# A planned matmul kernel on one core: first x tiles in half rows, w1 ahead of w2, and smaller steps for the sums

## The chip, the core and the metric

The kernel runs on one core of one Trainium2 chip, in one launch. The metric is the device time of that core in microseconds (us), as a median over runs. Three runs of the kernel before gave 298.87, 298.88 and 298.90 us.

The engines are named as the profile names them: PE does the matmuls and PEld its weight loads, DVE (VectorE), ACT (ScalarE) and POOL (GpSimd) work on tiles, SP and POOL issue the DMAs here.

## What is computed

```
x: 16 x 512 x 1024, w1 and w2: 1024 x 768, all float32
y1 = x @ w1 ; y2 = x @ w2
out = tanh(y1) * y2          (float32)
```

Flattened, x has 8192 rows, which are 64 tiles of 128 rows ("tile 0" to "tile 63").

## The kernel before

**Two ways to multiply.** The inner dimension of 1024 is cut into 8 chunks k of 128. The columns are cut into three blocks of 512: a is the first 512 columns of w1, b the first 512 of w2, and G the last 256 columns of both side by side. Tiles 0 to 3 ("the head") are multiplied plainly, 8 matmuls of 128x512 for each tile and block (line 522, `m0a4` for tile 0, block a, chunk 4). That makes 4 tiles x 2 blocks + 3 tiles x 1 block, 88 plain matmuls; block b of tile 3 is held back and done as 16 matmuls of 128x256 at the very end. Tiles 4 to 63 go in 20 triples. In a triple the three tiles, each cut in two halves of the inner dimension, and the six weight blocks (three column blocks by two halves) are combined by a fast scheme: 15 products `p0` to `p14` (line 550, 4 matmuls of 128x512 each) instead of 18. Its operands are sums of x blocks (`A_SUMS`, L16, formed by `x_sum`, L505, named `S34.0` for triple 0) and sums of weight blocks (`B_SUMS`, L20, formed once by `w_sum`, L493, named `B5`). The results are added up by `C_OPS` (L29): `copy` and `seed` on ACT, `add` on DVE, then tanh on ACT and the product with y2 on DVE.

**The head.** The loads are float32. `SP_LOADS` and `ACT_LOADS` (L97, L99) list their order: `y0` is the whole of x tile 0 (512 KB), `u3` chunk 3 of w1 (384 KB), `v3` chunk 3 of w2. Each is cast to float16 on DVE or ACT (`cast_y` L417, `cast_w` L431). The x tiles of the head and tiles 4, 5 and 6 are transposed on PE (L463, 8 transposes of 128x128 for each tile, 56 in all) and copied out of PSUM. Later x tiles are loaded as float16 by POOL's DMAs (L471) and transposed by DMAs that SP issues (L474).

**What sets the order.** The whole program is straight-line code. A class `Planner` (L103) takes every step as an `op` with the engines that may do it, a duration, what it needs and a due time, and plays the run forward; the order in which it starts the steps is the order in which the instructions are written, engine by engine. The order of the products is a list (`plan.strict`, L612, from `PE_ORDER` and `PE_HEAD`); the other due times are worked out backward from it. Since each engine takes its instructions in order, a step that comes late holds what stands behind it.

**Fillers.** Matmuls of constants (L857) keep PE busy before the first data (`WARM`, L90) and ahead of four named steps (`FILLERS`, L91).

**The guard.** ACT sums |x| of every tile and |w| of every chunk (`abs_sum`, L476; the x sums are `D0` to `D63`, L814 and L830). Five small steps (`f1` to `f5`, L844) turn the sums into a flag, and after the last product a branch takes a general path if an input is out of range; it is not taken here.

Of the kernel before, what the change touches and what calls it, by code (L numbers as in the profile page):

```python
# [17 lines left out]
    (51, 16, 35, "add"), (15, 11, 4, "sub"), (31, 16, 15, "sub"), (63, 31, 32, "add"), (21, 10, 31, "add"),  # L18
)
B_SUMS = (  # L20
# [5 lines left out]


# [51 lines left out]
PE_HEAD = ("1a0 0a1 1b1 0b1 1G1 p7 p1 0a0 3a0 2b1 p6 0G0 2a1 1b0 1G0 3a1 "  # L79
           "p10 3G1 0b0 p9 p12 2G1 p8 1a1 p11 p14 2b0 0G1 3G0 2G0 2a0")  # L80
# [9 lines left out]
WARM = (512, 512, 256)  # L90
FILLERS = {"PT1.0": (512,), "m1b2": (192,), "m1b7": (256,), "PT2.1": (448,)}  # L91
# [4 lines left out]
EARLY_LOADS = {0: 0.2}  # L96
SP_LOADS = ("y0 y1 v7 u3 y2 u1 v4 u0 v0 "  # L97
            "v1 v3 u2 u4 v5 v6 u6 u5 u7")
ACT_LOADS = "y3 v2"  # L99
POOL_LOADS = "5.0:v5 4.0 4.1 5.1 6"  # L100


class Planner:  # L103
# [221 lines left out]
    def spare(self, n):  # L325

        t = self.start_of[n]
        return [b for b in range(len(self.held)) if all(t <= a or z <= t - 1.0 for a, z in self.held[b])][0]
# [3 lines left out]
def kernel(  # L332
# [27 lines left out]
    XF_BUFS, XG_BUFS = 3, max((SP_LOADS + ACT_LOADS).count("y"), 1)  # L360
# [13 lines left out]
    xtpool = pool("xt", XT_BUFS)  # L374
    spool = pool("s", S_BUFS)
# [14 lines left out]
    xt_last = once.tile([P, KO, P], f16, name="xT_last")  # L390

# [6 lines left out]
    xgpool = head_stack.enter_context(tc.tile_pool(name="xg", bufs=XG_BUFS))  # L398
# [10 lines left out]
    x32, wfs, xhs, xts, ss, cs, os_ = {}, {}, {}, {}, {}, {}, {}  # L409

    def load_x32(e, mt, halves):
        if mt not in x32:
            x32[mt] = xfpool.tile([P, K], f32, tag="xf", name="x_f")
        at = slice(halves[0] * F, (halves[-1] + 1) * F)
        pin(engine[e].dma_start(x32[mt][:, at], xf[mt][:, at]))  # L415

# [30 lines left out]

    def xt_tile(mt):
        if mt not in xts:
            xts[mt] = xt_last if mt == HEAD - 1 else xtpool.tile([P, KO, P], f16, tag=f"xT{mt % 3}", name="xT")  # L450
        return xts[mt]

    def transpose_32(e, mt, h, chain):
        for k in range(KH):
            pin(nc.tensor.transpose(bank(chain)[:, k * P:(k + 1) * P], x32[mt][:, (h * KH + k) * P:(h * KH + k + 1) * P], ident))
# [16 lines left out]

    def transpose(e, mt):
        pin(nc.sync.dma_start_transpose(xt_tile(mt), xhs[mt]))  # L474
# [4 lines left out]
    def abs_x(e, mt):  # L479
        abs_sum(e, xhs[mt] if mt in xhs else x32[mt], mt)  # L480
# [11 lines left out]

    def w_sum(e, v, a, b, how):  # L493
# [5 lines left out]
    def x_operand(i, v):  # L499
        if v & (v - 1):  # L500
            return ss[i, v]
        bit = v.bit_length() - 1
        return xts[HEAD + 3 * i + bit // 2][:, bit % 2 * KH:(bit % 2 + 1) * KH, :]

    def x_sum(e, i, v, a, b, how):  # L505
        ss[i, v] = spool.tile([P, KH, P], f16, tag=f"s{v}", name=f"s{v}")
        pin(engine[e].tensor_tensor(ss[i, v], x_operand(i, a), x_operand(i, b), OP[how]))  # L507
# [11 lines left out]
    def mm(e, chain, mt, k, c, lo, n):  # L519
        begun[chain] = begun.get(chain, 0) + 1  # L520
        w = w_columns(k, c, lo, n)
        pin(nc.tensor.matmul(shaped(bank(chain)[:, lo:lo + n], w), xts[mt][:, k, :], w, start=begun[chain] == 1, stop=begun[chain] == KO, skip_group_check=True))  # L522

    def plain_tanh(e, mt, lo, n, chain):
        pin(nc.scalar.activation(out_tile(mt)[:, lo:lo + n], bank(chain)[:, :n], ACT.Tanh))
# [5 lines left out]
    def steady_pools(e):  # L531
        head_stack.close()
        steady["c"] = fast.enter_context(tc.tile_pool(name="c", bufs=C_BUFS, reuse_waits="tile"))

# [50 lines left out]
    def gate_x(e, mt):  # L585
        pin(nc.gpsimd.tensor_copy(held_x, xts[mt][:, 0, :1]))  # L586
# [8 lines left out]
    ACT_F, ACT_G, ACT_W, ACT_D, ACT_AW = (0.50, 0.59), (0.29, 0.38), (0.80, 0.86), (1.06, 1.26), (0.94, 1.04)  # L595
    PERIOD = 15 * SLOT
# [3 lines left out]
    head_at = {entry: HEAD_START + n * SLOT for n, entry in enumerate(head)}  # L600
    ORIGIN = HEAD_START + (len(head) - 15) * SLOT
# [25 lines left out]
    parts, early, last, back = {}, set(), "", []  # L627
    both = sorted([(ISSUE_ACT * z, "act", z, n) for z, n in enumerate(act_loads)] + [(ISSUE_SP * z, "sp", z, n) for z, n in enumerate(sp_loads)])
    issuer, last_on = {}, {"act": "", "sp": ""}
    for _, e, z, n in both:  # L630
# [3 lines left out]
        if n[1] == "y":  # L634
            mt = int(n[2])
            op(n, {e: (0.49, 0.49) if e == "sp" else (ISSUE_ACT, 0.5) if n != act_loads[-1] else (ISSUE_ACT + TABLE, 0.5)}, -100, [], load_x32, mt, (0, 1), issued=[last], behind=back[-WF_BUFS:][:1] if len(back) >= WF_BUFS else [],
# [3 lines left out]
            for h in range(2):  # L640
# [3 lines left out]
                early.add(f"T{mt}.{h}")  # L644
        elif n[1] == "x":
            z = n[2:]
            mt = int(z[0])
            halves = (int(z[2]),) if z[1:] else (0, 1)
# [7 lines left out]
        else:  # L656
            c, k = n[1], int(n[2])
            op(n, {e: (0.49, 0.49) if e == "sp" else (ISSUE_ACT, 0.5) if n != act_loads[-1] else (ISSUE_ACT + TABLE, 0.5)}, -100, [], load_w, c, k, issued=[last], behind=back[-WF_BUFS:][:1] if len(back) >= WF_BUFS else [],
               dma=(e, 0.985 + more, 1.15, 0.75, 0.121))
# [31 lines left out]
    def loads_of(mt):  # L691
        if mt not in parts:
            return [f"L{mt}"]
        return [n for n in sp_loads + act_loads if n[:3] in (f"Lx{mt}", f"Ly{mt}")] if mt < HEAD else ["L" + part(mt, k)[1:] for k in (0, KO - 1)]

    xt_readers = {mt: [] for mt in range(MT)}


    outs = {mt: [] for mt in range(MT)}
    for c in "aGb":  # L700
        for mt in range(HEAD):
            chain = (c, mt)
            if c == "b" and mt == HEAD - 1:
                continue
            last = []
            for n, k in enumerate(K_ORDER):
                w = [f"c{z}{k}" for z in {"a": "u", "b": "v", "G": "uv"}[c]]
                name = f"m{mt}{c}{k}"
                op(name, {"pe": (MM, MM)}, head_at[f"{mt}{c}{k // KH}"] + n % KH * MM, w + [part(mt, k)], mm, chain, mt, k, c, 0, F, chains=[chain])
                last.append(name)  # L710
            xt_readers[mt] += last
            due = max(head_at[f"{mt}{c}{h}"] for h in range(2)) + MUL_DUE
            if c == "a":
                op(f"th{mt}a", {"act": ACT_F}, due, last, plain_tanh, mt, 0, F, chain, chains=[chain])
            elif c == "G":
                op(f"th{mt}G", {"act": ACT_G}, due, last, plain_tanh, mt, F, G, chain, chains=[chain])
                op(f"mu{mt}G", {"dve": DVE_G}, due, last + [f"th{mt}G"], plain_mul, mt, F, G, chain, G, chains=[chain])
                outs[mt].append(f"mu{mt}G")
            else:
                op(f"mu{mt}b", {"dve": DVE_F}, due, last + [f"th{mt}a"], plain_mul, mt, 0, F, chain, 0, chains=[chain])  # L720
                outs[mt].append(f"mu{mt}b")
# [7 lines left out]
    def w_needs(v):  # L729
        return [f"B{v}"] if v in wsum else casts(v)  # L730

    for v, a, b, how in B_SUMS:
        op(f"B{v}", {"dve": DVE_B}, None, w_needs(a) + w_needs(b), w_sum, v, a, b, how)

    def x_needs(i, v):
        if v & (v - 1):
            return [f"S{v}.{i}"]
# [3 lines left out]
    op("pools", {"pool": (0.0, 0.0)}, 24, back + [f"D{mt}" for mt in range(HEAD)], steady_pools)  # L741
# [8 lines left out]
    for v, a, b, _ in A_SUMS:  # L750
        for u in (a, b):
            if u in a_readers:
                a_readers[u].append(f"S{v}")
# [12 lines left out]
    for i in range(TRIPLES):  # L766
        for v, a, b, how in A_SUMS:
# [212 lines left out]
```

## Time and profile before

| what | value |
|---|---|
| median of three runs | 298.88 us |
| profiled execution, first to last instruction (its span) | 297.3 us |
| PE busy | 290.9 us (98% of the span) |
| DVE busy | 255.5 us (86%) |
| ACT busy | 227.6 us (77%) |
| POOL busy | 46.7 us (16%) |
| HBM read / written | 39.85 MB / 25.17 MB |

The profile is of one execution, and its span of 297.3 us is the only time that it has of its own; the median of the timed runs is 1.6 us above it, which lies around the span. A change of the span is taken as the same change of the time. A busy PE is not a PE at its best: the matmul records overlap, so a matmul's rate is read from how far apart the starts are, not from its length, and constants count as busy.

### The profile page before, as it was taken

How to read it: one execution, taken by the hardware profiler on the slowest of the kernel's cores; microseconds unless marked ns; L12 is line 12 of the kernel's file. 1: busy time of each engine (PE TensorE's matmuls, PEld its weight loads, DVE VectorE, ACT ScalarE, POOL GpSimd, SP SyncE). 2: the span in 40 equal slices, each digit the busy share in tenths (PEclk: the TensorE clock that was granted, in tenths of full speed). 3: DMA queues.
4: the chain of work that ended last, by engine and by line, in shares of the span. 5: the costliest groups of instructions: out<-in, count | busy, mean ns of one | idle time of the engine just before them, and what ended most of it. 6: DMA issues, size and time to landing. Idle time of an engine off the chain costs nothing.

```text
span 297.3 us, 4698 instructions
## 1 busy us (share of the span) xinstructions
PE 290.9 (98%) x1419; PEld 137.7 (46%) x1419; DVE 255.5 (86%) x517; ACT 227.6 (77%) x450; POOL 46.7 (16%) x122
## 2 busy tenths in 40 slices
PE   6999999999999999999999999999999999999995
PEld 3545444444444675444444444444444444444443
DVE  1458999999988999898899988989899898999685
ACT  3798988996969769697876979788696866867561
POOL 1024040211030111113121010212101030000000
PEclk9999999999999999999999999999999999999999
DMA  7999999999999999999999999999989899681316
GB/s 263 406 403 230 162 169 222 242 251 258 110 317 212 221 255 244 221 215 259 161 227 217 172 223 199 246 224 215 226 169 245 164 279 244 144 240 47 119 55 215
DMA packets 82827, 64.55 MB, mean 217 GB/s; under 512 B 62704, under 2 KB 64752, under 8 KB 82800
## 3 DMA queue, kind: packets, MB, share of 16 engines
q1 hardware_dynamic: 73584, 47.59, 62.6%
q0 software_dynamic: 8928, 15.73, 34.3%
q10 hardware_dynamic: 288, 0.92, 0.8%
q8 instruction: 11, 0.18, 0.3%
q14 instruction: 16, 0.13, 0.1%
HBM read 39.85 MB, written 25.17 MB: 219 GB/s over the span
## 4 chain that ended last, share of the span: by engine, by line
PE 91%; DMA 6%; ACT 1%; SPq 0%; DVE 0%; issue 0%
PE bank L550 87%; DMA w_f<-in_w_dram 4%; PE bank L522 3%; DMA x_f<-in_x_dram 2%; ACT wh L427 1%; PE bank L463 1%; SPq L423 0%; DVE o_last L529 0%; SPq L415 0%; PE bank L580 0%
## 5 line engine op out<-in xcount | busy, mean ns | idle before, releaser
L550 PE MATMUL bank<-b,s 128*128 128x512 f16 (+1 forms) x664 | 148.1, 371 | 0.0
L550 PEld LDWEIGHTS <-s 128*128 128x128 f16 x832 | 81.2, 98 | 91.4 <-DVE s L507 0.6
L553 ACT ACTIVATE s<-bank 128x512 f32<-128x512 f32 x100 | 58.6, 595 | 41.0 <-PE bank L550 40.5
L560 DVE TENSOR_TENSOR bank<-bank,s 128x512 f32<-128x512 f32 x100 | 69.5, 697 | 18.1 <-PE bank L550 7.8
L477 ACT ACTIVATE junk<-xh 128x1024 f16<-128x1024 f16 x64 | 67.3, 1051 | 0.2
L567 DVE TENSOR_TENSOR o<-o,bank 128x512 f32<-128x512 f32 (+1 forms) x120 | 63.1, 548 | 2.5 <-ACT o L563 1.7
L550 PEld LDWEIGHTS <-xT 128*128 128x128 f16 x412 | 40.3, 98 | 46.1 <-ACT xT L427 0.2
L550 PE MATMUL bank<-b,xT 128*128 128x512 f16 (+1 forms) x252 | 58.5, 369 | 0.0
L563 ACT ACTIVATE o<-bank 128x256 f32<-128x256 f32 (+1 forms) x80 | 33.0, 432 | 12.4 <-PE bank L550 6.1
L550 PE MATMUL bank<-wh,s 128*128 128x512 f16 (+1 forms) x168 | 41.1, 369 | 0.0
L550 PE MATMUL bank<-wh,xT 128*128 128x512 f16 x160 | 40.9, 379 | 0.0
L586 POOL COPY held_x<-xT 128x1 f16<-128x1 f16 x52 | 12.2, 235 | 165.1 <-DMA xT<-xh 165.0
L471 POOL DMA_DIRECT2D xh<-in_x_dram x62 | 33.3, 540 | 20.3 <-issue 6.6
L507 DVE TENSOR_TENSOR s<-s,xT 128x512 f16<-128x512 f16 x80 | 32.3, 421 | 1.2
L563 ACT ACTIVATE o<-s 128x512 f32<-128x512 f32 x40 | 24.9, 623 | 1.2 <-DVE s L560 1.2
L507 DVE TENSOR_TENSOR s<-xT 128x512 f16<-128x512 f16 x60 | 25.0, 418 | 0.0
L553 ACT ACTIVATE bank<-bank 128x512 f32<-128x512 f32 x40 | 21.7, 573 | 1.6 <-DVE bank L560 0.9
L522 PE MATMUL bank<-wh,xT 128*128 128x512 f16 x72 | 18.8, 378 | 0.3
L507 DVE TENSOR_TENSOR s<-xT,s 128x512 f16<-128x512 f16 x40 | 16.7, 417 | 0.0
L560 DVE TENSOR_TENSOR bank<-s,bank 128x512 f32<-128x512 f32 x20 | 13.9, 694 | 1.6
L560 DVE TENSOR_TENSOR s<-s,bank 128x512 f32<-128x512 f32 x20 | 13.6, 681 | 0.3 <-ACT s L553 0.3
L477 ACT ACTIVATE junk<-wh 128x768 f16<-128x768 f16 x16 | 13.5, 842 | 0.2
(42 smaller groups left out, 120.6 us busy)
## 6 DMA issues: line engine op xcount, KB each, us to landing
out_dram<-o SPq DMA_DIRECT2D x54, 384.0 KB, 4.7
xh<-in_x_dram POOLq DMA_DIRECT2D x58, 256.0 KB, 5.7
w_f<-in_w_dram SPq DMA_DIRECT2D x15, 384.0 KB, 6.3
out_dram<-o SPq DMA_DIRECT2D x9, 256.0 KB, 2.0
x_f<-in_x_dram SPq DMA_DIRECT2D x3, 512.0 KB, 4.7
out_dram<-o SPq DMA_DIRECT2D x9, 128.0 KB, 1.7
xT<-xh SPq DMA_TRANSPOSE x57, 5.3
x_f<-in_x_dram ACTq DMA_DIRECT2D x1, 512.0 KB, 4.9
```

The lines of the kernel that those rows point to most:

```text
L427: pin(nc.scalar.copy(dst, src))
L463: pin(nc.tensor.transpose(b[:, (k - lo) * P:(k - lo + 1) * P], xhs[mt][:, k * P:(k + 1) * P], ident_h))
L471: pin(nc.gpsimd.dma_start(xhs[mt][:, lo * P:(lo + n) * P], xf[mt][:, lo * P:(lo + n) * P]))
L477: pin(nc.scalar.activation(junk[:, :src.shape[-1]], src, ACT.Abs, scale=scale, accum_out=sums[:, column:column + 1]))
L507: pin(engine[e].tensor_tensor(ss[i, v], x_operand(i, a), x_operand(i, b), OP[how]))
L522: pin(nc.tensor.matmul(shaped(bank(chain)[:, lo:lo + n], w), xts[mt][:, k, :], w, start=begun[chain] == 1, stop=begun[chain] == KO, skip_g ...
L550: pin(nc.tensor.matmul(to, x_operand(i, a)[:, k, :], w, start=begins and k == 0, stop=k == KH - 1, skip_group_check=True))
L553: pin(nc.scalar.activation(place(i, dst, True), place(i, src), ACT.Copy, scale=float(sign)))
L560: pin(nc.vector.tensor_tensor(d, a, b, ALU.add if signs == (1, 1) else ALU.subtract))
L563: pin(nc.scalar.activation(out_tile(HEAD + 3 * i + r)[:, lo:lo + n], place(i, src)[:, :n], ACT.Tanh, scale=float(sign)))
L567: pin(nc.vector.tensor_tensor(o, o, place(i, src)[:, at:at + n], ALU.mult))
L586: pin(nc.gpsimd.tensor_copy(held_x, xts[mt][:, 0, :1]))
```

## The change

**Loads.** Tiles 0 to 3 are loaded and cast in half rows: `h3.0` is the first half (chunks 0 to 3) of tile 3, 256 KB. There are 8 of them where there were 4 whole tiles. All 24 loads stand on SP's queue, none on ACT's. The chunks of w1 (u) come ahead of those of w2 (v) but for `v4`, `v7` and `v6`, and tile 2 comes late, behind `v6`.

**Columns.** Block G is no longer one matmul of 128x512 over both weights. Its w1 part is U and its w2 part is V, each 256 wide; a and U read chunks of w1 alone, b and V chunks of w2. Two tiles share a PSUM bank. This makes 64 matmuls of 128x256 out of 32 of 128x512.

**Sums of weights in halves.** `B5`, `B36`, `B37`, `B45` and `B29` are formed in two halves of 256 columns each; the first half needs w1 alone.

**Sums of x in pairs.** `S34` and `S10` are one instruction, `S35` and `S11` another; for that the x tiles and the sums of a triple lie in one tile each (`xTs0`, `ss0`).

**Late sums of |x|.** D0 to D3 are due from 70 us on. D4 to D8 are taken from a second load of tiles 4 to 8, issued on POOL after the last tile's transpose (5 more DMAs of 512 KB read).

**Block b of tiles 0 to 2** is copied out of its bank by ACT, and multiplied by tanh some 30 us later from SBUF.

**Order.** Due times of some 350 steps and the order of the first 41 products are now given as numbers (`DUES`, `FIRST`); the fillers are found by the planner from its own gaps up to its 24 us.

```diff
-PE_HEAD = ("1a0 0a1 1b1 0b1 1G1 p7 p1 0a0 3a0 2b1 p6 0G0 2a1 1b0 1G0 3a1 "
-           "p10 3G1 0b0 p9 p12 2G1 p8 1a1 p11 p14 2b0 0G1 3G0 2G0 2a0")
+PE_HEAD = ("0a1 1a1 2a1 3a1 0U1 1U1 2U1 3U1 0a0 1a0 2a0 3a0 0U0 1U0 2U0 3U0 "
+           "0b1 1b1 2b1 0V1 1V1 2V1 3V1 0b0 1b0 2b0 0V0 1V0 2V0 3V0 p1 p6 p10 p7 p9 p12 p8 p11 p14")
+A_PAIRS = ((34, 10), (35, 11))
+B_HALVES = (5, 36, 37, 29, 45,)
-WARM = (512, 512, 256)
-FILLERS = {"PT1.0": (512,), "m1b2": (192,), "m1b7": (256,), "PT2.1": (448,)}
-SP_LOADS = ("y0 y1 v7 u3 y2 u1 v4 u0 v0 "
-            "v1 v3 u2 u4 v5 v6 u6 u5 u7")
-ACT_LOADS = "y3 v2"
-POOL_LOADS = "5.0:v5 4.0 4.1 5.1 6"
+WARM = (512, 384)
+SP_LOADS = "h3.0 h1.1 h1.0 h0.0 u5 h3.1 h0.1 u7 u0 u1 u2 u4 v4 u3 u6 v7 v6 h2.0 h2.1 v0 v5 v3 v2 v1"
+ACT_LOADS = ""
+HEAD_D_AT, HEAD_D_STEP = 70.0, 9.0
+RELOAD = (4, 5, 6, 7, 8)
+PLAIN_COPY, PLAIN_AT = (0, 1, 2), 30.0
+POOL_LOADS = "4.0:v0 4.1 5.0 5.1 6"
+DUES = ("ch0.1:11.483 PT0.1:-8.806 T0.1:-19.918 ch1.1:-6.643 PT1.1:30.467 T1.1:4.785 cu4:-38.532 ch2.1:7.264 "
...
+    def fillers(self, until):
+        found, busy = {}, None
+        for n in sorted((n for n in self.ops if self.engine_of[n] == "pe"), key=lambda n: self.start_of[n]):
+            t = self.start_of[n]
+            if t > until:
+                break
+            if busy is not None and t - busy > 0.32 and self.spare(n):
+                found[n] = self.spare(n)[0], int((t - busy - 0.18) * 580) // 32 * 32
+            busy = t + self.ops[n]["engines"]["pe"][0]
+        return found
...
+    def load_h(e, mt, h):
+        x32[mt, h] = xfpool.tile([P, F], f32, tag="xf", name="x_f")
+        pin(engine[e].dma_start(x32[mt, h], xf[mt][:, h * F:(h + 1) * F]))
+    def cast_h(e, mt, h):
+        if mt not in xhs:
+            xhs[mt] = xgpool.tile([P, K], f16, tag="xh", name="xh")
+        copy(e, xhs[mt][:, h * F:(h + 1) * F], x32[mt, h])
...
+    def reload_x(e, mt):
+        again[mt] = xhpool.tile([P, K], f16, tag="xh", name="xh")
+        pin(nc.gpsimd.dma_start(again[mt], xf[mt]))
...
+    def w_sum_half(e, v, a, b, how, h):
+        parts_of = [z[:, :, h] if len(z.shape) == 4 else z[:, :, h * G:(h + 1) * G] for z in (wsum[v], w_block(a), w_block(b))]
+        pin(engine[e].tensor_tensor(*parts_of, OP[how]))
...
+    def x_sum(e, i, sums_of):
+        out, a, b = (x_operands(i, [z[n] for z in sums_of]) for n in range(3))
+        pin(engine[e].tensor_tensor(out, a, b, OP[sums_of[0][3]]))
...
-    def mm(e, chain, mt, k, c, lo, n):
+    def mm(e, chain, mt, k, c, lo, n, at, count):
         begun[chain] = begun.get(chain, 0) + 1
-        w = w_columns(k, c, lo, n)
-        pin(nc.tensor.matmul(shaped(bank(chain)[:, lo:lo + n], w), xts[mt][:, k, :], w, start=begun[chain] == 1, stop=begun[chain] == KO, skip_group_check=True))
+        col = N * (c in "bV") + F * (c in "UV") + lo
+        pin(nc.tensor.matmul(bank(chain)[:, at:at + n], xt_tile(mt)[:, k, :], wh[:, k, col:col + n], start=begun[chain] == 1, stop=begun[chain] == count, skip_group_check=True))
...
+    def plain_copy(e, mt, chain):
+        ys[mt] = steady["y"].tile([P, F], f32, tag="y", name="y")
+        pin(nc.scalar.copy(ys[mt], bank(chain)))
+    def plain_mul_copied(e, mt):
+        o = out_tile(mt)[:, :F]
+        pin(nc.vector.tensor_tensor(o, o, ys[mt], ALU.mult))
```

**Place 1: PE at the first plain matmuls.** In the kernel before (`xh` is a cast x tile, `xT` a transposed one, `wh` the cast weights, `ones` the constants), two whole tiles are transposed before these rows:

```order
L463 MATMUL bank5_82<-ident_h_93,xh_167 128x128
L522 LDWEIGHTS xT_151
L522 MATMUL bank6_83<-wh_95,xT_151 128x512
L857 MATMUL bank0_77<-ones_91 128x192
L522 LDWEIGHTS xT_182
L522 MATMUL bank7_84<-wh_95,xT_182 128x512
L857 MATMUL bank0_77<-ones_91 128x256
```

And in the changed kernel, with half tiles (`xTs2` holds tiles 0 to 2, `xT_last` is tile 3):

```order
L553 MATMUL bank3_77<-ident_h_90,xh_166 128x128
L1039 MATMUL bank0_74<-ones_88 128x352
L625 LDWEIGHTS xTs2_94
L625 MATMUL bank4_78<-wh_97,xTs2_94 128x256
L625 MATMUL bank5_79<-wh_97,xTs2_94 128x512
L553 LDWEIGHTS xh_137
L553 MATMUL bank6_80<-ident_h_90,xh_137 128x128
```

The first plain matmuls, a 256-wide one of U and a 512-wide one of a, now stand ahead of the transposes of the second halves of tiles 3 and 0.

**Place 2: PE between the first products of triple 0.** Before, plain matmuls of the head (L522) stand between the products (L550; `s15_394` is a sum of x, `b37_100` one of weights):

```order
L550 MATMUL bank6_83<-b5_97,s15_394 128x512
L522 LDWEIGHTS xT_216
L522 MATMUL bank7_84<-wh_95,xT_216 128x512
L522 LDWEIGHTS xT_last_94
L522 MATMUL bank2_79<-wh_95,xT_last_94 128x512
L550 LDWEIGHTS xT_388
L550 MATMUL bank1_78<-wh_95,xT_388 128x512
```

Now (L625 plain, L662 products, `ss0` the sums of triple 0):

```order
L625 MATMUL bank6_80<-wh_97,xT_last_91 128x256
L662 LDWEIGHTS xTs0_92
L662 MATMUL bank0_74<-wh_97,xTs0_92 128x512
L662 MATMUL bank4_78<-wh_97,xTs0_92 128x512
L662 LDWEIGHTS ss0_95
L662 MATMUL bank3_77<-b24_103,ss0_95 128x512
L662 MATMUL bank7_81<-b5_99,ss0_95 128x512
```

All plain matmuls but those held for the end stand ahead of the first product, and nothing plain is left between products.

**Place 3: DVE ahead of the sum S15 of triple 1**, which product `p6` of that triple reads. Before (`s15_526`; `s34_517` is S34 of triple 1):

```order
L507 TENSOR_TENSOR s11_508<-s3_493,xT_402 128x512
L507 TENSOR_TENSOR s34_517<-xT_418,xT_385 128x512
L567 TENSOR_TENSOR o_467<-o_467,bank4_81 128x256
L507 TENSOR_TENSOR s15_526<-s11_508,xT_402 128x512
L497 TENSOR_TENSOR b45_102<-b37_100,wh_95 128x2048
```

Now (the rows of 128x1024 are pairs, `45_104` of 128x4x256 is a half sum of weights, and the last row is S15):

```order
L610 TENSOR_TENSOR ss1_96<-xTs1_93 128x1024
L589 TENSOR_TENSOR b45_104<-b37_102,wh_97 128x4x256
L610 TENSOR_TENSOR ss1_96<-ss1_96,xTs1_93 128x1024
L672 TENSOR_TENSOR bank0_74<-bank4_78,s56_518 128x512
L679 TENSOR_TENSOR o_485<-o_485,bank2_76 128x256
L679 TENSOR_TENSOR o_485<-o_485,bank1_75 128x512
L610 TENSOR_TENSOR ss1_96<-ss1_96,xTs1_93 128x512
```

S15 now stands behind an add and two output products, where one output product of 256 columns stood before.

More of the change, by code (lines that the diff above doesn't have):

```diff
@@ L479, in abs_x @@
     def abs_x(e, mt):
[L480 removed]
+        abs_sum(e, again[mt] if mt in again else xhs[mt], mt)
     def abs_w(e, t, k):
@@ L868 @@
             o = plan.ops[n]
-            for z in FILLERS.get(n, ()):
-                constants(banks[plan.spare(n)], z)
+            if n in fillers:
+                b, z = fillers[n]
+                for at in range(0, z, F):
+                    constants(banks[b], min(F, z - at))
             o["fn"](plan.engine_of[n], *o["args"])
```

208 lines of the change are left out of this document (146 added, 62 removed), and 45 rows, old and new, of the table DUES.

## The prediction

> **What bounds the kernel now.** I read the page first: busy shares, and the span in 40 slices.
>
> ```profile
> PE 290.9 (98%) x1419; PEld 137.7 (46%) x1419; DVE 255.5 (86%) x517; ACT 227.6 (77%) x450; POOL 46.7 (16%) x122
> PE   6999999999999999999999999999999999999995
> DVE  1458999999988999898899988989899898999685
> PEclk9999999999999999999999999999999999999999
> ```
>
> PE is the bound from end to end, but for the first slice of 7.4 us; DVE is nearly full from 22 us on. Then the chain of waits, in order of time:
>
> ```profile
> 22.98 3.40 PE bank L522 x15
> ...
> 31.16 2.59 PE bank L550 x12
> 33.75 1.08 PE bank L522 x5
> 34.83 0.94 PE bank L550 x4
> 35.77 0.86 PE bank L522 x4
> 36.63 242.78 PE bank L550 x1168
> ...
> 292.38 1.76 PE bank L522 x16
> ```
>
> From 23 us on PE waits for nothing worth counting. The 1168 are 1124 matmuls of 512 columns, since 44 of triple 5 are written as two halves (L547): 242.78/1124 = 0.216 us each. The last 16 are 256 wide: 1.76/16 = 0.110. So the change can win only ahead of 23 us, and lose anywhere. The timeline of that stretch:
>
> ```profile
> 0.98 0.86 SPq L415 DMA_DIRECT2D x_f<-in_x_dram  x2
> 1.30 3.92 PE L857 MATMUL bank<-ones 128*128 128x512 f32 x6 [1.30 <-DVE ones L853]
> 5.70 1.04 ACT L427 CAST xh<-x_f 128x1024 f16<-128x1024 f32 x1 [2.51 <-DMA x_f<-in_x_dram]
> 6.80 1.07 PE L463 MATMUL bank<-ident_h,xh 128*128 128x128 f16 x16 [1.59 <-ACT xh L427]
> 7.70 1.08 PE L857 MATMUL bank<-ones 128*128 128x512 f32 x2
> 8.70 0.62 PE L463 MATMUL bank<-ident_h,xh 128*128 128x128 f16 x8
> 9.16 0.38 PE L522 MATMUL bank<-wh,xT 128*128 128x512 f16 x1
> 10.05 0.56 DVE L429 CAST wh<-w_f 128x768 f16<-128x768 f32 x1 [0.27 <-DMA w_f<-in_w_dram]
> 10.50 1.02 PE L522 MATMUL bank<-wh,xT 128*128 128x512 f16 x4
> 24.12 0.56 DVE L429 CAST wh<-w_f 128x768 f16<-128x768 f32 x1 [0.90 <-DMA w_f<-in_w_dram]
> 31.00 1.03 PE L550 MATMUL bank<-wh,xT 128*128 128x512 f16 x4
> ```
>
> And the DMA side, in stretches of 5 us:
>
> ```profile
> 5.00:10.00 5.00, 3.41 (x32) 2.21 (x31) 2.71 (x5) 3.48 (x6) 0.00 (x0) 1.00 1.03 416
> 10.00:15.00 5.00, 4.87 (x27) 2.42 (x26) 1.31 (x3) 3.81 (x5) 0.00 (x0) 1.00 1.02 400
> 15.00:20.00 5.00, 5.00 (x24) 2.15 (x23) 2.26 (x3) 4.66 (x9) 0.00 (x0) 1.00 1.03 401
> ```
>
> The loads stream at 406 GB/s (mean of the last column), and the last weight chunk is ready at 24.12. So 8.39 MB (2.10 of head x, 6.29 of weights) set the pace, and a piece that ends B MB into the stream is ready near 24.1 - (8.39 - B)/0.406. For the fourth weight chunk on the queues (B = 2.75) this gives 10.2; its row says 10.05.
>
> **How much PE loses ahead of the products.** A transpose costs (1.07 - 0.62)/8 = 0.056. The first product starts at 31.00; the chain shows 9 of the 88 plain matmuls behind it. So 79 x 0.216 + 56 x 0.056 = 20.2 us of useful work stand in 31.0 us: 10.8 lost. By 10.50 it had done 24 transposes and 2 matmuls, 1.8 us: 8.7 lost. The other 2.1 go between 10.5 and 31 in waits and fillers.
>
> **Half rows, and w1 first.** The first 256 KB end 0.79 MB before the first two whole tiles did (two queues, 1.05 MB): 1.9 us earlier than 5.70, at 3.8. The cast of half a tile lies between 1.04/2 and 1.04; I take 0.6, so PE transposes at about 4.5 in place of 6.80. The first w1 chunk is fifth (B = 1.44): ready at 7.0, cast by 7.5. The second (B = 2.36) is ready at 9.2, cast by 9.8. Until then PE has 24 transposes and one chunk for three tiles, 1.34 + 3 x (0.216 + 0.110) = 2.3 us: 7.5 lost by 9.8. From there each chunk of 0.39 MB takes 0.97 us to land and brings 3 x 0.326 = 0.98 us of work, so PE can run full. How much it waits until its products has no row: at least 0 by that balance, at most about the 2.1 of before. I take 1.2, the middle and a little, since tile 2 comes late and casts stand in line:
>
> ```profile
> L427 ACT CAST wh<-w_f 128x768 f16<-128x768 f32 x10 | 8.3, 831 | 1.0 <-DMA w_f<-in_w_dram 0.4
> L429 DVE CAST wh<-w_f 128x768 f16<-128x768 f32 x6 | 3.4, 559 | 5.1 <-DMA w_f<-in_w_dram 5.1
> ```
>
> ACT's 0.83 is just under the 0.97 between chunks. Lost 8.7 in all, then. The plain work is 56 x 0.216 + 64 x 0.110 + 3.1 = 22.2, which prices U and V: 64 x 0.110 - 32 x 0.216 = 0.1. The first product starts at 30.9, with all 88 done. Before, 9 x 0.216 = 1.9 us were left at 31.0. **PE is 2.0 us ahead.**
>
> The Trainium skill (DMA: Bandwidth & Descriptors, section Bandwidth, Measured) says to batch DMAs to 1 MiB, with 32% of peak at 64 KB and 78% at 1 MB; an estimate of 55% for 256 KB pieces would make 2.1 MB of half rows some 3 us longer, and the sum about 301. The rows above speak against it as far as they go, since 384 KB chunks stream at the full rate.
>
> The queue: all 24 loads are now issued by SP, 4 more than before on both queues, and the transposes by DMA stand behind them.
>
> ```profile
> 6.99 11.15 SPq L423 DMA_DIRECT2D w_f<-in_w_dram  x13
> 30.15 9.29 SPq L474 DMA_TRANSPOSE xT<-xh  x4
> ```
>
> SP's last load was issued near 18 and its first transpose at 30.15, so 12 us cover the longer list; without that cover it would be four issues of about 0.4. Nothing on SP is waited for in between. The three copies of block b cost ACT 3 x 0.6, and fall where four sums of |x| (4 x 1.24, below) have left it: nothing.
>
> **What the middle takes back.** Products now follow each other from the first. Before, nine plain matmuls stood between them (place 2), and hid copies, adds and sums. DVE has little to spare there:
>
> ```profile
> 30.00:36.00 6.00, 6.00 (x29) 2.65 (x28) 5.96 (x12) 5.93 (x11) 0.53 (x1) 1.00 1.28 174
> 36.00:48.00 12.00, 12.00 (x57) 5.39 (x56) 11.76 (x24) 10.14 (x20) 3.73 (x8) 1.00 1.18 174
> 48.00:60.00 12.00, 12.00 (x57) 5.43 (x56) 11.48 (x23) 10.46 (x23) 2.15 (x6) 1.00 1.10 239
> L497 DVE TENSOR_TENSOR b<-wh 128x2048 f16<-128x2048 f16 x6 | 7.2, 1222 | 0.4 <-ACT wh L427 0.2
> L507 DVE TENSOR_TENSOR s<-xT 128x512 f16<-128x512 f16 x60 | 25.0, 418 | 0.0
> L529 DVE TENSOR_TENSOR o<-o,bank 128x512 f32<-128x512 f32 x3 | 2.0, 680 | 0.0
> ```
>
> The columns of the stretches are PE, PEld, DVE, ACT, POOL. DVE is idle for 0.04 + 0.24 + 0.52 = 0.8 us in 30 us. The change moves three 0.68 us multiplications out (2.0) and part of the weight sums to before 25 us, where DVE is idle. A half sum (1024 elements) lies between 0.42 and 1.22, by the line through both 0.69; ten halves for five sums add 0.8. A pair has the same size, 0.69 for 2 x 0.42, and saves 0.3 in each triple. So DVE is relieved, but not of its order: at place 3 S15 stands behind an add and two output products, and `p6` waits for it with nothing plain to run in between. The loss lies between 0 and the whole cover of 1.9; I take half, 0.95.
>
> **What the tail takes back.** Sums of |x| lie on ACT:
>
> ```profile
> L477 ACT ACTIVATE junk<-xh 128x1024 f16<-128x1024 f16 x64 | 67.3, 1051 | 0.2
> L477 ACT ACTIVATION_READ_ACCUMULATOR junk<-xh 128x1 f32 x64 | 12.4, 193 | 0.0
> 250.00:280.00 30.00, 30.00 (x142) 13.62 (x140) 27.52 (x61) 19.06 (x38) 0.72 (x2) 1.00 0.56 153
> ```
>
> Five of them move from 30 to 50 us to the last 40, where ACT is busy 19.06 of 30 us: room for 5 x 1.24 = 6.2. But each holds a copy behind it for up to 1.05, and a product may wait for that copy. Bounds 0 and 1.0 (one full hold); I take 0.3, since most copies are made in time. The four of tiles 0 to 3 move from before 25 us to 70 and later, hidden by PE's products; uncovered they would cost a hold each. The five reloads and POOL's issues lie at the same place, where DMA is busy 0.56: nothing.
>
> **Sum:** -2.0 + 0.95 + 0.3 = -0.75. From 298.88, 298.1 us; a span of 296.5.
>
> **The rivals.** The measurement of this kernel can tell 0.2%, 0.6 us, from no change.
> - The lead is kept whole: nothing of the middle is lost. For it: only 0.1 us of waits show after 36 us now. Against: the cover is gone. 297.0. Chance 0.09.
> - The lead is given back: the middle takes all 1.9. For it: DVE's 0.8 us of idle time. 299.1, no change. Chance 0.22.
> - DVE can't follow (slower). If half sums cost more than about 1.0, ten add over 4 us to a queue with 0.8 to spare and 2.0 freed; PE then loses its lead and 1 us or more by 60 us: 300.2. Against: 2048 elements at 1.22 show no such fixed cost. Chance 0.07.
> - Half rows stream slower: each holds the queue as long as a 384 KB chunk, 0.97 for 0.65, and 8 x 0.32 = 2.6 us come on top: 300.7. The rule on batching above is of this kind. Chance 0.04.
> - The clock rises later. The same weight load of the warm-up gets shorter at 4.6 us:
>
> ```profile
> 2.31 0.34 PEld L857 LDWEIGHTS bank<-ones 128*128 128x128 f32 x1 [0.52 <-issue]
> 4.62 0.19 PEld L857 LDWEIGHTS bank<-ones 128*128 128x128 f32 x1 [0.26 <-issue]
> ```
>
> The warm-up is now shorter (896 constant columns for 1280), with gaps behind it. If the half clock lasted to 9.8, 24 transposes (1.34) and some 700 filler columns at 1.0 us per 512 (1.4) would take 2.7 more, about 1.5 of it in free gaps: 1.2 later, 299.3. Chance 0.06. The Trainium skill (TensorE: Matmul & The Clock Gate, Part 1) has the clock rise after one busy window of about 3.4 us that runs freely; the trace agrees, 3.3 us after the first constants at 1.30 at the latest, and shows nothing of a later rise.
>
> **How the numbers follow.** My forecast has 0.52, and 0.44 of that lies beyond 0.6 us; with the lead kept, faster is 0.53. Same is 0.08 of the forecast, 0.22 and half of the clock's 0.06: 0.33. Slower is 0.07, 0.04 and 0.03: 0.14. The range: waits before 31 us may be 0 to 2.1, the middle 0 to 1.9, the tail 0 to 1.0; not all at one end at once, so 0.8 below and 1.1 above, which also takes in the lead given back: 297.3 to 299.2.
>
> **What would show it.** First transpose at 4.3 to 4.8; first product at 30.5 to 31.5 with no plain matmul behind it until the end; gaps of PE between 31 and 50 us of 0.5 to 1.4 in sum, ahead of `p6` above all; 0 to 1.0 near 270. Plain matmuls that stall for casts after 10 us, or a half sum over 0.8, would make it wrong.

## The result, and the profile after

The changed kernel is slower. Four runs gave 303.47, 304.26, 308.04 and 311.78 us; the four of the kernel before beside them gave 298.87 to 300.17, median 298.89. The ratio is 1.0155, 95% interval 1.0115 to 1.0195; it leaves out the two longest runs, which lie over 1.5% above the shortest. So there are two findings to explain: some 5 us more even in a good run, and a spread of 8 us between runs where the kernel before has 1.3.

The profiled execution took 304.26 us with a span of 302.6, 5.3 above the span before. First the chain of waits of the changed kernel (start, length, what), some of its pieces:

```profile
3.31 5.49 DMA x_f<-in_x_dram
8.88 7.46 DMA w_f<-in_w_dram
16.41 8.06 DMA w_f<-in_w_dram
24.49 0.84 ACT wh L506
25.38 2.65 PE bank L625 x15
...
36.94 7.97 PE bank L662 x36
...
46.02 208.48 PE bank L662 x1008
...
263.83 6.06 DMA xTs<-xh
...
278.83 6.20 PE bank L662 x28
...
295.42 1.76 PE bank L625 x16
```

Before, PE carried the chain from 23 us to the end. Now loads carry it to 24.5 us, and it leaves PE again around 37 and 46 us and for 24 us from 254.5 on, with a transpose by DMA of 6.06 us in it. Four places, then, each held against the kernel before by the starts of PE's matmuls.

**The head: +0.2.** The first product starts at 33.18 us with no plain matmul left behind it; before, at 31.00 with nine left (1.9 us), which is 32.9. From the timeline of after (start, length, engine, instruction, idle time ahead of it and what ended that):

```profile
3.62 0.62 ACT L506 CAST xh<-x_f 128x512 f16<-128x512 f32 x1 [1.35 <-DMA x_f<-in_x_dram]
4.45 0.63 PE L553 MATMUL bank<-ident_h,xh 128*128 128x128 f16 x4
5.67 0.62 ACT L506 CAST xh<-x_f 128x512 f16<-128x512 f32 x1 [0.62 <-DMA x_f<-in_x_dram]
7.24 0.62 ACT L506 CAST xh<-x_f 128x512 f16<-128x512 f32 x1 [0.95 <-DMA x_f<-in_x_dram]
8.18 0.56 DVE L508 CAST wh<-w_f 128x768 f16<-128x768 f32 x1 [0.27 <-DMA w_f<-in_w_dram]
```

The stretch from 5 to 10 us in the table of stretches (its bounds and length; busy us of PE, PEld, DVE, ACT, POOL; clock, DMA share, GB/s):

```profile
5.00:10.00 5.00, 4.60 (x29) 3.19 (x28) 1.90 (x5) 2.88 (x6) 0.00 (x0) 1.00 0.99 340
```

The first transpose on PE comes as early as forecast (4.45), but then half rows, due every 0.65 us, come 1.24 and 1.57 apart, the first weight chunk at 8.18, and this stretch moves 340 GB/s (last column) where it moved 416 before.

**The middle: +0.9.** Gaps of PE of 0.29 at 36.9 us, 0.42 at 46.0, 0.12 at 50.5 and 0.03 at 38.8. The largest ends with a sum of x, S15 of triple 1, as its row in the timeline shows; the gap at 36.9 ends with an add (L672), which was done at 36.89:

```profile
46.02 4.49 PE L662 MATMUL bank<-b,ss 128*128 128x512 f16 x20 [0.26 <-DVE ss L610]
```

**The tail: +2.1.** PE's waits from 250 to 290 us (us in all, times, longest); in the kernel before this view is empty there:

```profile
PE bank L662 <- DVE bank L672: 0.8, 1, 0.8
PE bank L662 <- ACT bank L665: 0.5, 1, 0.5
PE bank L662 <- DVE o L679: 0.2, 1, 0.2
```

The stretch from 250 to 280 us, in the columns of the table above:

```profile
250.00:280.00 30.00, 28.45 (x131) 12.69 (x130) 24.00 (x49) 21.54 (x43) 3.36 (x7) 1.00 0.91 202
```

By the starts of the matmuls the gaps are 1.00 at 267.4, 0.64 at 273.2, 0.40 at 278.8. The DMA share of the stretch is 0.91 where it was 0.56. **The end: +2.3.** From the start of the last matmul to the end of the span it was 3.4 us, and is 5.7. SP's waits from 292 us on show where:

```profile
SPq L618 <- DVE o L679: 3.4, 5, 1.6
SPq L1160 <- DMA out_dram<-o_last: 2.3, 1, 2.3
SPq L1160 <- PEq L1160: 0.7, 2, 0.5
```

The same view of the kernel before, without its last row of 0.2 us:

```profile
SPq L515 <- DVE o L567: 1.4, 2, 1.0
SPq L975 <- PEq L975: 0.7, 2, 0.5
```

The wait for the DMA of `o_last` is new: the last output lands 3.77 us after its issue, before 1.71. The four places add up to 5.5 against 5.3 in the span. In this execution PE has no gap between 51 and 267 us; the longer runs must have lost their time somewhere else.

### The profile page after: what moved, and what is told of

It is laid out like the page before. It is cut to its first block, busy times and chain, and to the rows that moved or that the text cites. A ratio compares the mean times of both kernels' runs of the same rounds, so it can differ in the third digit from the quotient of the medians.

```text
span 302.6 us, 4745 instructions
## 1 busy us (share of the span) xinstructions
PE 292.7 (97%) x1453; PEld 141.6 (47%) x1453; DVE 249.2 (82%) x480; ACT 233.2 (77%) x459; POOL 48.9 (16%) x127
## 4 chain that ended last, share of the span: by engine, by line
PE 80%; DMA 9%; DVE 4%; ACT 2%; SPq 2%; issue 1%; DVEq 0%
PE bank L662 77%; DMA w_f<-in_w_dram 5%; PE bank L625 2%; DVE ss L610 2%; DMA xTs<-xh 2%; DMA x_f<-in_x_dram 2%; SPq L568 1%; ACT junk L571 1%; DVE bank L672 1%; ACT o L675 1%; DVE s L672 1%; SPq L489 1%; PE bank L553 0%; DVE o L679 0%; ACT xTs L506 0%
## 5 line engine op out<-in xcount | busy, mean ns | idle before, releaser
L662 PE MATMUL bank<-b,ss 128*128 128x512 f16 (+1 forms) x664 | 148.0, 371 | 1.5 <-DVE bank L672 0.8
L662 PEld LDWEIGHTS <-ss 128*128 128x128 f16 x832 | 81.2, 98 | 93.6 <-issue 2.4
L672 DVE TENSOR_TENSOR bank<-bank,s 128x512 f32<-128x512 f32 x100 | 69.6, 697 | 21.5 <-ACT o L675 14.4
L662 PEld LDWEIGHTS <-xTs 128*128 128x128 f16 x412 | 40.2, 98 | 46.9 <-issue 0.8
L662 PE MATMUL bank<-b,xTs 128*128 128x512 f16 (+1 forms) x252 | 58.5, 369 | 0.5 <-ACT bank L665 0.5
L662 PE MATMUL bank<-wh,ss 128*128 128x512 f16 (+1 forms) x168 | 40.9, 369 | 0.0
L662 PE MATMUL bank<-wh,xTs 128*128 128x512 f16 x160 | 40.8, 379 | 0.0
L610 DVE TENSOR_TENSOR ss<-ss,xTs 128x512 f16<-128x512 f16 (+1 forms) x60 | 30.6, 510 | 1.0
L610 DVE TENSOR_TENSOR ss<-xTs 128x512 f16<-128x512 f16 (+1 forms) x40 | 21.0, 550 | 3.2 <-DMA xTs<-xh 3.0
L625 PE MATMUL bank<-wh,xTs 128*128 128x256 f16 (+1 forms) x96 | 20.1, 325 | 0.8 <-ACT wh L506 0.7
L610 DVE TENSOR_TENSOR ss<-xTs,ss 128x512 f16<-128x512 f16 x40 | 16.7, 417 | 0.0
L672 DVE TENSOR_TENSOR s<-s,bank 128x512 f32<-128x512 f32 x20 | 13.6, 680 | 0.8 <-ACT s L665 0.6
L672 DVE TENSOR_TENSOR s<-bank,s 128x512 f32<-128x512 f32 x20 | 13.6, 682 | 0.4 <-ACT s L665 0.4
L672 DVE TENSOR_TENSOR bank<-s,bank 128x512 f32<-128x512 f32 x20 | 13.8, 689 | 0.1
```

The lines of the kernel that those rows point to most:

```text
L610: pin(engine[e].tensor_tensor(out, a, b, OP[sums_of[0][3]]))
L625: pin(nc.tensor.matmul(bank(chain)[:, at:at + n], xt_tile(mt)[:, k, :], wh[:, k, col:col + n], start=begun[chain] == 1, stop=begun[chain] ...
L662: pin(nc.tensor.matmul(to, x_operand(i, a)[:, k, :], w, start=begins and k == 0, stop=k == KH - 1, skip_group_check=True))
L672: pin(nc.vector.tensor_tensor(d, a, b, ALU.add if signs == (1, 1) else ALU.subtract))
```

## The experiments

Theories at the start: the half rows stream slowly (head), the second loads of tiles 4 to 8 collide with the last transposes (tail), against rivals that blame the single queue and the sums on ACT.

**Whole rows** (e1), **no second loads** (e2), **both** (e3), **second loads held back** (e4).

```
e1  load_h: one dma_start of xf[mt] for both halves, none at the second; three buffers of 4 KB
e2  reload_x: again[mt] = xhs[MT - 1], no dma_start
e3  both
e4  + op("gateR", {"pool": ...}, None, [f"T{MT - 1}"], gate_x, MT - 1, issued=[pool_last])   # ahead of the second loads
```

> The changed kernel with tiles 0 to 3 loaded as whole rows of 4 KB (one load of 512 KB at the place of a tile's first half, none at the second); casts, transposes and all orders stay. Theory (half rows stream slower): the stretch from 4 to 8 us moved 255 GB/s where whole rows moved 400, so the six early halves cost about 2 us; the first product starts near 31.2 us in place of 33.18, and the kernel is 1.5 to 2 us faster than the changed one (profiled 302.5 for 304.3). Rival (one queue in place of two, or the order of the loads, makes the head late): the first product stays at 33, no change of time.

> The changed kernel without the five second loads of tiles 4 to 8 on POOL; the five sums of |x| stay where they are and read the resident tile 63 instead (so tiles 4 to 8 are left out of the guard). Theory (the second loads collide with the last transposes by DMA, since nothing on the chip holds POOL until the last transpose): PE's 2.1 us of gaps from 265 to 279 us fall to 0.4 or less, the last transpose lands in under 4 us, time 1.7 us below the changed kernel's. Rival (the sums on ACT hold the copies): the gaps stay at 1.5 us or more. If the second loads also make the spread of 303.5 to 311.8 us between runs, the spread falls below 1 us.

> Both edits of the two runs before: whole rows and no second loads (tiles 4 to 8 left out of the guard). If both theories hold the gains add up: 3.5 to 3.8 us below the changed kernel, about 300.5; what is left above the kernel before is the 0.9 us of gaps from 33 to 51 us. If either rival holds, only the other's gain is left.

> The changed kernel with a one-column copy of the transposed tile 63 on POOL ahead of the second loads, so that they are held until the last transpose has landed. Theory (collision): as without the second loads, PE's gaps from 265 to 279 us fall to 0.6 or less, 1.5 us faster than the changed kernel; the sums end by 285 us and the flag after them is not late. Rival (the sums on ACT cost the time, wherever the loads are): gaps of 1.5 us or more remain, only later.

Medians: e1 303.71 (303.01 to 306.03), e2 310.02 (302.75 to 312.68), e3 302.09 (300.35 to 311.41), e4 304.04 (302.54 to 306.56); before 299.13 (298.65 to 301.62) in the same session. No median falls by what was expected; the spread hides the gains, so the places are read from the profiles. The spread stays without the second loads: that part of the theory fell.

e1 starts its first product at 32.27 (0.9 earlier, half of what was expected), and its last weight lands at 25.16, where it was 26.37 in the changed kernel and 24.09 before. (The stretch from 4 to 8 us that e1's expectation puts at 255 GB/s moved 284.) So whole rows give back about half of what the loads lost. What takes the other half isn't shown; the single queue, one of the rivals, was tested in no run by itself.

In e2, e3 and e4 the gaps after 265 us are 0.25 in all, where e1, which keeps the second loads, has 1.4. The last three transposes (tiles 61 to 63) took 13.6, 7.1 and 6.1 us to land in the changed kernel, 6.5, 3.2 and 3.1 in e4, and 5.9, 3.1 and 3.5 before. e2 keeps the sums on ACT and loses the gaps all the same. The tail is the collision.

The profile of e2 happens to be of a long execution (311.62 us; the shortest took 302.75), and shows where it lost its time: seven gaps of PE from 55 to 181 us add up to 9.0 us. DVE's waits from 60 to 250 us, and one of the places in its timeline:

```profile
DVE bank L671 <- ACT o L674: 10.4, 11, 1.3
DVE ss L609 <- DMA xTs<-xh: 9.0, 5, 2.8
DVE ss L609 <- issue: 4.8, 2, 3.0
```

```profile
127.80 2.07 SPq L567 DMA_TRANSPOSE xTs<-xh  x1
...
134.48 1.03 DVE L609 TENSOR_TENSOR ss<-xTs 128x1024 f16<-128x1024 f16 x2 [2.77 <-DMA xTs<-xh]
...
136.49 0.69 DVE L671 TENSOR_TENSOR bank<-bank,s 128x512 f32<-128x512 f32 x1
...
138.35 0.68 DVE L678 TENSOR_TENSOR o<-o,bank 128x512 f32<-128x512 f32 x1
...
139.08 1.02 PE L661 MATMUL bank<-wh,xTs 128*128 128x512 f16 x4 [1.86 <-DVE o L678]
```

At 134.48 DVE begins the pair S34 and S10 after 2.77 us of idle time: the pair reads all three x tiles of the triple. The third was issued for transposition at 127.80 and landed at 134.36; the second had landed at 131.07. Adds and output products stand behind the pair on DVE, and PE waits 1.86 us for one of them. In the rows of before, S3, S11 and S15 came first, which need two tiles; S31, the first that reads the third, came 4 us later. From landing to first use a third tile had 7.4 us (median of the rows from 60 to 250 us, lowest 3.8), and now has 2.1 (lowest 0.1), while a transpose takes anything from 3 to 13 us. That is a new theory: not DMA traffic as such, but the order that the pairs force.

**The order turned round in both kernels** (h1, h2), **the code of the path not taken** (h4), **half rows in the kernel before** (k1).

```
h1  17 of the 20 triples on DVE: S34+S10, S3, S35+S11, .., S15  ->  S3, S11, .., S15, S34+S10, S35
h2  kernel before, triples 3 to 18: S3, S11, S15, .., S34, .., S10  ->  S3, S34, S10, S11, S15, ..
h4  h1, and in general_path: range(KO) -> range(KO // 2) in the products
k1  kernel before, load_x32: for h in halves: one dma_start per half row
```

> The changed kernel with the sums of x on DVE in another order in each triple: S3, S11 and S15 first (S11 alone), then the pair S34 with S10, then S35 alone; one instruction more in each triple, all else the same. Theory (the pairs let the row's first sum wait for the third x tile, whose DMA transpose lands at a time that varies): a third tile's time from landing to first use rises from 2.1 us (median, after 60 us) to 5 or more, PE has no gap over 0.1 us from 60 to 250 us in the profile, the runs lie within 1 us of each other, and the median falls from 304 to 306 down to 302 to 303. Rival (the spread comes from the DMA traffic, the second loads or the single queue): the runs still spread over 3 us or more.

> The kernel before, no pairs, with S34 and S10 of triples 3 to 18 moved ahead of S11 on DVE: the same instructions in another order, so that the second sum of a row needs the third x tile. Theory (order of the sums): the third tile's time from landing to first use falls from 7.4 to about 3.8 us, PE gets gaps of 0.3 to 2 us at changing places between 60 and 250 us, runs spread over 2 us or more and the median rises by 0.5 to 3 us. Rival (the spread has to do with something else in the change): runs stay within 0.5 us of 298.9.

> As the run before, and the path that is not taken is shortened: its products go over half of the inner dimension, 32 PE instructions less in the program and none less executed. Theory (PE's jump over that path now lands in a piece of code that has to be loaded, 16 KB on a DMA engine that the last output needs, while before it did not): no code load on its queue after 290 us, the last output lands 1.7 us after its issue in place of 3.7, and the kernel is 2.0 us faster than the run before. Rival (the last output is late for another reason, such as the order of the stores): no change.

> The kernel before with each of the four loads of x tiles 0 to 3 split into two loads of half rows on the same queue, nothing else. Theory (half rows are slow at the start): packets of 2 KB with 400 to 800 ns show from 3 to 8 us, as in the changed kernel, the stretch moves 250 to 300 GB/s in place of 400, the last weight lands 1 to 2 us later than 24.09, time 299.5 to 301. Rival (something else in the changed head slows the loads): within 0.3 us of 298.9.

h1 missed: 308.74 (307.77 to 309.69). These five runs lie within 2 us, but h4, with the same sums in the same order, has one of 315.26. PE now has a gap of about 0.3 to 0.6 in nearly every row, since S34 and S35 stand ahead of adds that PE waits for. So this order moved more than the third tile's first use, and it tells nothing on the median. h2 is the clean test: the same instructions in another order took the quiet kernel from 298.87 (17 runs, 298.68 to 299.34) to 299.74 (12 runs, 298.97 to 305.16), ratio 1.0039 (1.0017 to 1.0061); the third tile's margin fell from 7.4 to 3.2 (lowest 0.0), and a wait shows on DVE that the kernel before does not have:

```profile
DVE s L507 <- DMA xT<-xh: 1.6, 2, 0.8
```

So the order alone costs 0.9 us in the median, and its runs spread over 6 us where those of the kernel before beside them spread over 0.7. It is not the only source of spread: in two other sessions the kernel before has runs of up to 301.62 and 305.04.

k1 gave 301.99 (one run), 3.1 above the kernel before. Two of its stretches, and the same two of the kernel before:

```profile
3.00:5.00 2.00, 2.00 (x4) 0.80 (x3) 0.00 (x0) 0.00 (x0) 0.00 (x0) 1.00 0.94 296
5.00:8.00 3.00, 0.94 (x3) 0.21 (x1) 0.69 (x1) 2.04 (x2) 0.00 (x0) 1.00 0.99 355
```

```profile
3.00:5.00 2.00, 2.00 (x5) 0.87 (x3) 0.00 (x0) 0.19 (x1) 0.00 (x0) 1.00 1.01 395
5.00:8.00 3.00, 1.41 (x18) 1.16 (x18) 1.17 (x3) 1.81 (x3) 0.00 (x0) 1.00 1.02 412
```

The last weight lands at 26.21 in place of 24.09: half rows cost 2 us of the loads. The first product comes 2.7 later (33.69), and a gap of 0.33 at 41.1 is new; together that is nearly all of the 3.1. What stretched 2.1 to 2.7 isn't isolated, but in this execution the clock of PE also rose late. Its weight loads of constants, two to a row, show when:

```profile
12.70 0.76 PEld L859 LDWEIGHTS bank<-ones 128*128 128x128 f32 x2
13.68 0.41 PEld L859 LDWEIGHTS bank<-ones 128*128 128x128 f32 x2
```

In the kernel before, whose warm-up is the same, one such load takes 0.34 at 4.02 and 0.19 at 4.62.

h4 differs from h1 in nothing that is executed. Its last output lands in 1.73 us (h1: 3.31), with 11 loads on the code queue in place of 12, and from the last matmul to the end it takes 3.7 us in place of 5.3; the median is 1.2 lower, where 2.0 was expected.

**All causes undone** (h5: order alone; h8: with held second loads and shorter code; h6: with whole rows; h7: with the longer warm-up).

```
h5  triples 3, 5 to 18:  S3, S11, S15, S31, S63, S34+S10, S35
h8  h5, e4's gate; general_path: transposes by DMA, G of both weights in one matmul (32 PE instructions less)
h6  h8, e1's whole rows        h7  h6, WARM = (512, 512, 256)
```

> The changed kernel with the sums of x in a row once more in another order, now so that DVE's other steps keep their places: S3 and S11 alone first, the pair S34 with S10 and S35 alone only behind S63, in triples 3 and 5 to 18; nothing else. Theory (pairs first make every row wait for its third tile): no gap of PE over 0.1 us from 100 to 250 us, also none of the regular kind that the first reordering brought; runs within 1.5 us of each other; median 303 to 304, since tail and end are as in the changed kernel. Rival (the spread has another source): 3 us or more between runs.

> As the run before, and two more edits: the second loads of tiles 4 to 8 wait on POOL until tile 63 has been transposed, and the path that is not taken is written with 32 PE instructions less. Half rows are kept. Theory: the three causes add up, 1.3 to 2.1 us in the tail and 1.6 to 2.0 at the end; median 300.0 to 300.8, runs within 1.5 us. Rival (the gains overlap, or the held loads delay the flag): 301.5 or more.

> As the run before, with whole rows for tiles 0 to 3 in place of half rows. Theory (small packets at the start): the first product starts 0.7 to 1 us earlier and the median is lower by as much, 299.2 to 299.9; what then is left above 298.9 is the 0.9 us of gaps between 33 and 51 us, less the lead. Rival (the rows don't matter, the order of the loads does): no change beyond 0.2 us.

> As the run before, with the longer warm-up of the kernel before (1280 columns of constants for 896). Theory that the later rise of the clock (7.1 us for 4.3) costs nothing, since PE waits for loads until 9.8 us: no change beyond 0.2 us, though the clock rises before 5 us. Rival: 0.3 to 1.2 us faster.

Medians: h5 305.10 (four runs 303.05 to 305.92, two of 313.17 and 320.42), h8 301.48 (300.93 to 303.70), h6 299.66 (298.85 to 303.16), h7 299.70 (298.79 to 305.77).

h5: the third tile has some 7 us again, and PE no gap between 100 and 250 us. The gaps left in the four profiles are at 55 to 65 us and one at 95, where PE or DVE also waits for a transpose; triples 0 to 2, 4 and 19 keep the old order. That is what the profiles show. The runs show no cure of the spread: two of the six lie above every run of the changed kernel, and no trace of such a run exists.

h8 came out 0.7 above its expected range, at the edge of the rival's 301.5, and h6 within its own. Whole rows are worth 1.8 in the medians, with the first product at 32.46 for 33.76. Over all profiles the first product of the changed kernel's versions starts between 33.18 and 34.48 with half rows (seven profiles) and between 32.22 and 32.71 with whole rows (five), so half rows also add to the spread, and the profile of the changed kernel, at 33.18, is their luckiest.

h7 changes nothing in the median, but its theory wasn't put to the test: two weight loads of constants still take 0.45 at 6.05 us and 0.30 only at 6.85, while in h6 they take 0.30 from 5.36 on. The longer warm-up came with a later clock here, not an earlier one.

**Each cause alone in the quiet kernel** (n2: code, n3: second loads), and **the middle** (n1).

```
n2  kernel before, general_path: for t in (0, 1, 0, 1, 0, 1): the products three times over
n3  kernel before, + 5 x op(f"R{mt}", {"pool": ...}, ..., reload_x, mt, issued=[pool_last], ...)    # no sums
n1  h6, S15.1 ahead of m2.0, th1.0 of copy56.1, seed56.1 of copy60.0, D12 of th0.0, add64.0 of S63.0, copy191.1 of seed16.0
```

> The kernel before with the path that is not taken made longer (its products are written three times over, 128 PE instructions more in the program, none more executed). Theory (PE's jump lands in a piece of code that has to be loaded while the last output is written): a twelfth load on the code queue at the end, the last output lands 3.2 to 3.8 us after its issue in place of 1.7, time 298.87 + 1.5 to 2.0 = 300.4 to 300.9. Rival (the end is late in the changed kernel for a reason of its own): 298.9, no change.

> The kernel before with the five second loads of tiles 4 to 8 on POOL behind its last load, as the changed kernel has them, but with no sums on them: nothing reads what they bring. Theory (they share the DMA engines with the last two transposes, since POOL runs ahead of SP): the transposes of tiles 62 and 63 take 2 us more or longer to land, PE gets gaps of 1 to 2.2 us near 270, time 299.9 to 301. Rival (the sums on ACT are what costs the tail): 298.9 within 0.3 us.

> The version with all causes undone and whole rows, and six steps on DVE and ACT between 28 and 50 us moved ahead of a few others (S15.1 ahead of m2.0, copies and seeds ahead of tanh steps and of a sum of |x|). Theory (the gaps from 33 to 51 us come from the order on DVE and ACT): the 0.9 us of gaps there fall to 0.5 or less, median 299.66 - 0.5 = 299.1 to 299.3, the fastest run near 298.4, below the kernel before. Rival (the gaps come from late data): no change.

n2: 300.89 (eight runs 300.19 to 301.39, two of 306.06 and 444.29), ratio 1.0047 (1.0029 to 1.0065) to 299.13 in that session. The last output lands in 3.74 us, and SP's wait at the end is back:

```profile
SPq L975 <- DMA out_dram<-o_last: 2.1, 1, 2.1
```

The queue that loads code has one load from 290 to 303 us, at 296.1, the twelfth in the execution (packets, MB, share):

```profile
q8 instruction: 1, 0.02, 0.4%
```

All 17 profiles agree: the eight with twelve loads on that queue take 5.1 to 5.7 us from the last matmul to the end, the nine with eleven take 3.4 to 3.7.

n3: 306.88 (304.06 to 308.69), ratio 1.023 (1.0189 to 1.027), far more than expected. The last transposes take 14.5, 11.6 and 8.7 us to land, and PE waits:

```profile
PE bank L554 <- ACT bank L557: 4.0, 1, 4.0
PE bank L554 <- DVE bank L564: 1.2, 1, 1.2
```

The stretches around the longer of these waits:

```profile
272.00:275.00 3.00, 0.36 (x2) 0.09 (x1) 1.10 (x3) 0.00 (x0) 0.00 (x0) 1.00 1.05 343
275.00:276.00 1.00, 0.00 (x0) 0.00 (x0) 1.00 (x3) 0.27 (x1) 0.00 (x0) 0.82 0.46 174
276.00:279.00 3.00, 2.64 (x7) 0.96 (x7) 2.97 (x9) 1.60 (x4) 0.00 (x0) 0.50 0.00 0
279.00:282.00 3.00, 3.00 (x16) 1.30 (x15) 2.78 (x7) 1.58 (x3) 0.00 (x0) 0.99 0.46 164
```

PE all but stands still from 272 to 276 us, and then the clock (the column ahead of the DMA share) is at 0.50 for 3 us: 7 matmuls from 276 to 279. So this stall was paid for twice, the second time with about 1.5 us (7 x 0.21). No sums were on these loads, so the rival that blames ACT is out. The size of the collision varies: in the profiles that have the second loads unheld, the gaps of PE after 250 us add up to 0.4 (h5) to 2.1 us (the changed kernel), and to 7.1 in n3.

n1: 299.11 (298.41 to 301.05), ratio 0.9999 (0.998 to 1.0017). The gaps of the middle fell from 0.86 in h6 to 0.51; the median fell by 0.55, which is not clear of the noise between two sessions. It ties with the kernel before and doesn't beat it; its shortest run is 0.3 shorter. Its profile (of a run of 299.95) shows why: PE is 0.7 ahead at the first product (32.22 for 32.9) and loses 0.5 in the middle and 0.3 near 277. It also has two gaps, of 0.54 and 0.63 us at 153 and 158. The first ends with a copy on ACT behind a sum that had waited 1.0 us for a load of x. The second follows a wait in a row of the new order: there the first tile took 15.5 us to land, and DVE waited 2.0 us even for S3, which reads that tile alone. The order of the sums doesn't protect a row against a transpose as late as that.

## Why the prediction was wrong

It forecast 298.1 in 297.3 to 299.2; the shortest run was 303.5. By its steps:

- **"The first 256 KB ... at 3.8; PE transposes at about 4.5."** Right: 4.45.
- **"A piece that ends B MB into the stream is ready near 24.1 - (8.39 - B)/0.406."** Failed. The rate was taken from loads with rows of 3 and 4 KB, on two queues, and put on rows of 2 KB on one. The first weight chunk was ready at 8.15, not 7.0, the second at 10.47, not 9.2. The lead of 2.0 was in fact -0.2. The rival "half rows stream slower" had named this, at a chance of 0.04, with the right evidence against it: late half rows (two at 20 us) do land 0.67 us apart, at full rate. Only the early ones are slow. They are not the whole of it: with whole rows (e1) the first weight chunk lands at 8.96, and for its B of 1.97 the formula gives 8.3. (In the prediction's check of the formula the chunk with B = 2.75 is the third weight chunk, not the fourth; the times are right.)
- **"The first product starts at 30.9."** 33.18. The lost time ahead of it is 33.18 - 22.2 = 11.0, against 8.7.
- **The middle, 0.95.** Right in size (0.86 between 36 and 51 us) and half in cause: 0.42 of it is `p6` of triple 1 waiting for S15, as forecast; the 0.29 at 36.9 waits for an add of triple 0. n1 took 0.35 away by order alone.
- **"A pair ... saves 0.3 in each triple."** Right as a duration, wrong as a price. The step asked how long a pair takes and not what it waits for: the third tile, 4 us earlier than before. In the one trace of a long run (e2) such waits are where nearly all of its 9.0 us of gaps come from, and h2 shows that the order alone costs time; it can't be seen in an execution whose transposes happen to be quick, such as the profiled one. That it is the whole of the spread isn't shown: versions in the new order still have long runs.
- **"The five reloads and POOL's issues lie at the same place, where DMA is busy 0.56: nothing."** Failed: 2.1 us in place of 0.3 in the profile, and a median 7.7 higher in n3. A mean share of 0.56 over 30 us says nothing on the 10 us in which four loads and three transposes meet. And the reloads did not stand behind the last transpose, as the section on the change has it: nothing held POOL, which issued them from 252.5 us on, while SP issued the last transpose at 263.8.
- **The end** was in no term: "64 matmuls of 128x256 out of 32" was priced as PE time (0.1) and not as code. PE runs 1453 matmuls where it ran 1419, and as many more weight loads, and the end took 2.3 us longer.
- **The clock** did rise later: matmul-transposes at 4.45 and 5.73 us take 0.63 for four, and 0.40 from 7.91 on. The forecast put nothing on it and left it to a rival; whether it cost anything here stays open, since h7 did not bring the rise forward.

Still open: what makes early half rows slow (most of their packets take 84 ns, as at 20 us, but of 495 that begin from 3 to 8 us 19 take over 300, up to 786, and no run says why), what else holds the loads back when the rows are whole, what part of the spread is left when the order is put right, and what stretched 2.1 us of loads to 3.1 in k1.

## What to carry to other kernels

Price a step by what it waits for as well as by how long it takes: joining two operations moves the earlier one behind the operands of both, and if one comes by a DMA whose landing varies by 10 us, the margin that is lost can show as spread between runs and be missing from a profile. Where loads are added at a place with spare bandwidth, look at what else is in flight in just those microseconds, and hold the queue by a real wait if the order matters. A rate may be carried over only between transfers of the same shape at the same place.

## What the runs showed of the hardware

- Code that is not executed can cost time: with 128 more PE instructions in the path not taken (n2) a twelfth 16 KB load appears on the code queue just as the last output is written, and that output lands 2 us later (3.74 for 1.71); with 32 fewer (h4 against h1) the load is gone and the output lands after 1.73 in place of 3.31. The medians move by +1.8 and -1.2 us.
- After PE had stood still for 4 us, its clock was at half for 3.4 us (n3).
- Loads of half rows (2 KB per row) moved 261 GB/s from 3 to 5 us and 295 from 5 to 8, where whole rows moved 395 and 412 in the kernel before; at 20 us half rows landed at the full rate, 256 KB in 0.67 us.
- A transpose by DMA landed after 3.1 us in a quiet place (before, tile 62) and after 14.5 with four loads of 512 KB beside it (n3, tile 61). In the middle of a kernel, with only the usual loads beside it, 15.5 occurred once too (n1, at 138 us).
- The same warm-up of constants let the clock rise at 4.6 us in one execution (before) and at 13.7 in another (k1, with half rows).
